# A layer's second feed-forward block: its left sums read the whole normalised activation from copies instead of rejoining its two parts

## The chip, the cores and the metric

The kernel runs on one core of a Trainium2 chip. Its time is the device time of one execution in microseconds (us). The core has a matrix engine (TensorE, PE in the profile), a vector engine (VectorE, DVE), a scalar engine (ScalarE, ACT), a general engine (GpSimd, POOL), and SyncE (SP), which here only issues DMAs, one after the other. Each engine works through its own instructions in a fixed order; an instruction that must wait for another engine or for a DMA holds up all that stand behind it on its engine.

## The reference

One decoder layer for 1024 tokens of width 1024 in float32. The second feed-forward block, cut out of the whole, is

```
h = modulate(rms_norm(x, ffn2_norm[l]), sh3, sc3)
x = x + 0.5 * g3[:, None, :] * swiglu(h, ffn2_w_gate[l], ffn2_w_up[l], ffn2_w_down[l])
return rms_norm(x, final_norm)
```

with `modulate(h, shift, scale) = h * (1 + scale) + shift` and `swiglu(h, wg, wu, wd) = (silu(h @ wg) * (h @ wu)) @ wd`, and 2816 hidden channels. Ahead of it stand a first block of the same form and a mixer (a gated convolution and a state-space model) whose output projection ends in the kernel's w_out.

## The kernel before

The tokens are worked on in two halves of 512 (h = 0 and 1), the width in 8 k-tiles of 128. A tile of 128x512 float32 is 256 KB. Every factor of a matrix product is split into a high part hi (rounded to the matrix engine's short float32 form, fp32r) and a low part lo = value − hi, and one product of two tiles is three matmuls, hi·hi, hi·lo and lo·hi (`mm3`). ScalarE makes the hi parts (a cast), VectorE the lo parts (a subtraction).

The hidden channels are 11 groups of 256. Group 0 of the second block (`group0`, names fb0g for gate products, fb0u for up products) uses plain products, because it can start on half 0 while half 1 is still being normalised. Groups 1 to 10 (`seven`, names fb1g, fb1u and so on) multiply a 2x2 block matrix by seven products in place of eight. The left blocks are A11 and A12 (half 0, k-tiles 0 to 3 and 4 to 7), A21 and A22 (half 1, likewise), and four sums: S1 = A21 + A22, S2 = S1 − A11, S3 = A11 − A21, S4 = A12 − S2. The sums are made once and then serve ten groups.

The sums are made by `combos` and `combos_last`, on VectorE, from the parts of h: each block's tile is first made whole again by adding hi and lo (`whole`, names f, and s for S2), then added or subtracted, then split into hi (ScalarE, names h3S) and lo (VectorE). That is 9 VectorE instructions for each of four k, and 4 more for S4, 52 in all, with 16 casts on ScalarE. Before that `modulated` makes h for each k-tile and half: VectorE computes t = x · scale · 1/rms, ScalarE writes hi = t + shift, and VectorE writes lo = (t + shift) − hi in one three-operand instruction (SCALAR_TENSOR_TENSOR).

`seven("fb1", ...)` calls, after its first product (fb1gA, with A11), the down projection of group 0: `down2`, names fb0d. It has 16 outputs of 128x512, each of two `mm3`, 96 matmuls together. Each output stands in one of a few PSUM banks until VectorE has added it to the residual stream (`x <- fb0d, gate, x`); only then is the bank free for a later output. After fb0d come fb1gC (with S1), fb1gB (S2), fb1gD (S3), fb1gA (A12), fb1gE (A22) and fb1gC again (S4).

What sets the order: `Clock` counts the `mm3` issued and lets side work, the generators `combos` among it, advance by a step every few of them; an instruction scheduler then puts each engine's instructions in a final order. `Weights` loads weights in pieces of 1 MB (names raw), in order, as buffers come free; ScalarE casts a piece and VectorE makes its low part (names w). The temporaries of 128x512 (t, f, s and others) come from one pool (`t2k`) of six buffers used in turn. DMAs are all issued by SP in program order.

Of the kernel before, what the change touches and what calls it, by code (L numbers as in the profile page):

```python
# [13 lines left out]
F32 = mybir.dt.float32  # L14
F32R = mybir.dt.float32r
I32 = mybir.dt.int32
AF = mybir.ActivationFunctionType
ALU = mybir.AluOpType
# [3 lines left out]
P = 128  # L22
D = 1024
S = 1024
HALF = 512
# [207 lines left out]
def hymba_layer(ctx: ExitStack, tc, x_d, wm1_d, wmod_d, gu1_d, gs1_d, ds1_d, wl1_d, win_d, wout_d, glu_d, gu2_d, gs2_d, wd2_d, ds2_d, wl2_d, cols_d, cond_d, lam_d, bc_d, out_d):  # L233
    nc = tc.nc
    V, A, T, SP = (InOrder(tc, e) for e in (nc.vector, nc.scalar, nc.tensor, nc.sync))

    def pool(name, bufs=1, **kw):
        return ctx.enter_context(tc.tile_pool(name=name, bufs=bufs, **kw))
# [5 lines left out]
    scratch = pool("scratch", space=DRAM)  # L244
# [8 lines left out]
    def mov(name, where="A", shape=(P, 2, HALF), dtype=F32R):  # L253

        return movs[where].tile(list(shape), dtype, tag="m", name=name)
# [13 lines left out]
    def t2k(name):  # L269
        return tmp.tile([P, HALF], F32, tag="t", name=name)  # L270
# [47 lines left out]
    clock = Clock(4)  # L318
# [24 lines left out]
    def parts(name, where="A"):  # L343
        t = mov(name, where)
        return t[:, 0, :], t[:, 1, :]

    def split_act(src, name, where="A"):
        hi, lo = parts(name, where)
        A.copy(hi, src)
        V.tensor_tensor(out=lo, in0=src, in1=hi.bitcast(F32), op=ALU.subtract)  # L350
        return hi, lo
# [65 lines left out]
    def spread(rb, nm):  # L417
        bc = ps(nm + "bc")
        for i in range(rb.shape[1]):
            T.matmul(bc[:, i * P : (i + 1) * P], lhsT=rb[:, i, :], rhs=ident[:], start=True, stop=True)  # L420
        return bc

    def modulated(k, h, bc, n, name, where="A"):

        t = t2k(f"{name}t{k}_{h}")
        hi, lo = parts(f"{name}{k}_{h}", where)
        sh = mods[:, n, k : k + 1]
        V.scalar_tensor_tensor(out=t[:], in0=x[k][h], scalar=scl[:, n, k : k + 1], in1=bc[:], op0=ALU.mult, op1=ALU.mult)
        A.activation(hi, t[:], AF.Identity, bias=sh)
        V.scalar_tensor_tensor(out=lo, in0=t[:], scalar=sh, in1=hi.bitcast(F32), op0=ALU.add, op1=ALU.subtract)  # L430
        return hi, lo

    def norm_into(act, h, ss, n, name, where="A"):


        def use(bc):
            got = []
            for k in range(KT):
                clock.after(k, lambda k=k: got.append(modulated(k, h, bc, n, name, where)))
            act[h] = got  # L440

        ss.rstd(D, use, 8)
# [131 lines left out]
    blocks = {}  # L574


    def whole(pair, name, engine=nc.gpsimd):
        t = t2k(name)
        engine.tensor_tensor(out=t[:], in0=pair[0].bitcast(F32), in1=pair[1].bitcast(F32), op=ALU.add)
        return t  # L580

    def combos(act, name, homes):

        blocks.clear()
        while act[1] is None or len(act[1]) < KT:
            yield
        (a11, a12), (a21, a22) = [(act[h][:4], act[h][4:]) for h in range(2)]
        blocks.update(A11=a11, A12=a12, A22=a22, S1=[], S2=[], S3=[], S4=[])
        for k in range(4):
            f22, f21, f11 = whole(a22[k], f"f22_{k}", V), whole(a21[k], f"f21_{k}", V), whole(a11[k], f"f11_{k}", V)  # L590
            V.tensor_tensor(out=f22[:], in0=f21[:], in1=f22[:], op=ALU.add)
            blocks["S1"].append(split_act(f22[:], f"{name}S1_{k}", homes[0]))
            yield
            V.tensor_tensor(out=f21[:], in0=f11[:], in1=f21[:], op=ALU.subtract)
            V.tensor_tensor(out=f11[:], in0=f22[:], in1=f11[:], op=ALU.subtract)
            blocks["S2"].append(split_act(f11[:], f"{name}S2_{k}", homes[1]))
            yield
            blocks["S3"].append(split_act(f21[:], f"{name}S3_{k}", homes[2]))
            yield

    def combos_last(act, name, home):

        while "S3" not in blocks or len(blocks["S3"]) < 4:
            yield
        for k in range(4):
            f12, s2 = whole(act[0][4 + k], f"f12_{k}", V), whole(blocks["S2"][k], f"s2_{k}", V)
            V.tensor_tensor(out=f12[:], in0=f12[:], in1=s2[:], op=ALU.subtract)
            blocks["S4"].append(split_act(f12[:], f"{name}S4_{k}", home))
            yield

    SEVEN = (("A11", "A"), ("S1", "C"), ("S2", "B"), ("S3", "D"), ("A12", "A"), ("A22", "E"), ("S4", "C"))
# [224 lines left out]
    for h in range(2):  # L836
        bc = spread(rbs[h], f"p{h}")
# [10 lines left out]
    for k in range(KT):  # L848
# [4 lines left out]
        sh = mods[:, 0, k : k + 1]  # L853
        for h in range(2):
            hi, lo = parts(f"h1{k}_{h}")
# [353 lines left out]
    def after1(d, h):  # L1209
        n2[h].add(x[d][h], beside=d < 6)  # L1210
        if d == KT - 1:
            norm_into(act2, h, n2[h], 1, "h2")
# [298 lines left out]
    n3 = [Sumsq(f"n3{c}", home=acc_in_mov) for c in "ab"]  # L1511
    act3 = [None, None]
# [43 lines left out]
    mods_open.close()  # L1556
    es2.close()
    movs["B"] = ctx.enter_context(tc.tile_pool(name="movB", bufs=12))
    norm_into(act3, 0, n3[0], 2, "h3", "B")
    ws.retire(ring1)  # L1560
    for ds in ((4, 5), (6, 7)):
        w_out(ds, 1, 0)
        w_out(ds, 1, 1)
        ws.free(2)
    norm_into(act3, 1, n3[1], 2, "h3", "A")
    ring1_open.close()


# [4 lines left out]
    def group0():  # L1573

        a_tiles, pg, pu = {}, {}, {}
        g0, u0, g1 = ws.take(3)
        ready(act3, 0, KT)
        pg[0, 0], pu[0, 0] = proj(g0, act3[0], "fb0g0_0"), proj(u0, act3[0], "fb0u0_0")
        gu_evac(0, 0, pg[0, 0], pu[0, 0], a_tiles, "fb0_0_0")
        pg[1, 0] = proj(g1, act3[0], "fb0g1_0")  # L1580
        ready(act3, 1, KT)
        pg[0, 1] = proj(g0, act3[1], "fb0g0_1")
        ws.free()
        pu[0, 1] = proj(u0, act3[1], "fb0u0_1")
        gu_evac(0, 1, pg[0, 1], pu[0, 1], a_tiles, "fb0_0_1")
        ws.free()
        pg[1, 1] = proj(g1, act3[1], "fb0g1_1")
        ws.free()
        (u1,) = ws.take()
        for h in range(2):  # L1590
            gu_evac(1, h, pg[1, h], proj(u1, act3[h], f"fb0u1_{h}"), a_tiles, f"fb0_1_{h}")
        ws.free()
        return a_tiles

    clock.side.extend([combos(act3, "h3", "BAA"), combos_last(act3, "h3", "A")])
    a_prev = group0()
    kept = {g: kept_for(g, g not in LAST[1], True) for g in range(1, NGRP - 1)}
    HOMES = dict(A11="B", S2="A", A12="B", S3="A", S1="B", A22="A", S4="A")
# [132 lines left out]
```

## Time and profile before

| | us |
|---|---|
| median of 3 timed runs (lowest, highest) | 1735.42 (1735.38, 1735.46) |
| the profiled execution | 1740.78 |
| its span, from the first to the last instruction | 1739.0 |
| TensorE busy | 1665.4 (96%) |
| VectorE busy | 1273.6 (73%) |
| ScalarE busy | 596.7 (34%) |
| GpSimd busy | 375.9 (22%) |
| granted TensorE clock, mean over the span | 0.987 |

Line numbers say little here: nearly all instructions are recorded by a helper at L108, so groups are told apart by the names of their tiles, written out<-in with buffer numbers left out. The second feed-forward block starts at about 1066 us (fb0g, half 0); its half 1 starts at 1079 (fb0g), group 0's down projection fb0d at 1114.37, and fb1gC at 1145.84. In a timeline row the first number is the start and the second the length; in brackets stands how long the engine had been idle and who released it. A row of windows gives, for a stretch of time, the busy time and the instructions of TensorE's matmuls, its weight loads, VectorE, ScalarE and GpSimd, then the granted clock, the share of the DMA engines in use, and GB/s.

### The profile page before, as it was taken

How to read it: one execution, taken by the hardware profiler on the slowest of the kernel's cores; microseconds unless marked ns; L12 is line 12 of the kernel's file. 1: busy time of each engine (PE TensorE's matmuls, PEld its weight loads, DVE VectorE, ACT ScalarE, POOL GpSimd, SP SyncE). 2: the span in 40 equal slices, each digit the busy share in tenths (PEclk: the TensorE clock that was granted, in tenths of full speed). 3: DMA queues.
4: the chain of work that ended last, by engine and by line, in shares of the span. 5: the costliest groups of instructions: out<-in, count | busy, mean ns of one | idle time of the engine just before them, and what ended most of it. 6: DMA issues, size and time to landing. Idle time of an engine off the chain costs nothing.

```text
span 1739.0 us, 20621 instructions
## 1 busy us (share of the span) xinstructions
PE 1665.4 (96%) x7484; PEld 1368.4 (79%) x7484; DVE 1273.6 (73%) x2014; ACT 596.7 (34%) x1016; POOL 375.9 (22%) x290
## 2 busy tenths in 40 slices
PE   4999999999999999999999999999999999999997
PEld 3787788878878878787777778778888888888886
DVE  7939699997589997634556977967777766676656
ACT  4225433333364332331113414424444443322221
POOL 0012233322322222100000022123223322333211
PEclk9999999999999999999999999999999999999998
DMA  8222464554464656134655450114445334659312
GB/s 326 78 99 91 146 217 150 158 183 150 182 224 147 230 198 238 53 98 142 198 152 155 134 182 25 49 49 157 167 187 186 152 145 170 248 236 365 119 49 97
DMA packets 98167, 275.17 MB, mean 158 GB/s; under 512 B 18961, under 2 KB 34577, under 8 KB 86930
## 3 DMA queue, kind: packets, MB, share of 16 engines
q1 hardware_dynamic: 98066, 273.86, 44.8%
q8 instruction: 59, 0.97, 0.2%
q14 instruction: 42, 0.34, 0.1%
HBM read 194.65 MB, written 74.97 MB: 155 GB/s over the span
## 4 chain that ended last, share of the span: by engine, by line
PE 46%; DVE 7%; DMA 3%; issue 1%; ACT 0%; SPq 0%; POOL 0%; DVEq 0%; ACTq 0%
PE wo L108 2%; PE fb10d L108 2%; PE u L108 2%; PE fbd_1B L108 2%; PE fbd_0B L108 2%; PE b L108 2%; DMA swz<-si 1%; PE v L108 1%; PE fb0g L108 1%; PE fbd_1C L108 1%; PE fbd_0C L108 1%; PE fbd_1A L108 1%; PE fbd_0A L108 1%; DVE x L108 1%; DMA wm<-in_wmod 1%; PE gl L108 1%
## 5 line engine op out<-in xcount | busy, mean ns | idle before, releaser
L108 ACT CAST w<-raw 128x512 fp32r<-128x512 f32 (+1 forms) x374 | 240.4, 677 | 475.8 <-issue 79.4
L108 DVE TENSOR_TENSOR w<-raw,w 128x512 fp32r<-128x512 f32 (+1 forms) x374 | 306.6, 839 | 122.3 <-ACT w L108 121.7
L174 POOL TENSOR_TENSOR raw<-sums,raw 128x512 f32<-128x512 f32 x54 | 80.4, 1490 | 416.4 <-DVE w L108 404.0
L165 POOL TENSOR_TENSOR sums<-raw 128x512 f32<-128x512 f32 x54 | 77.4, 1434 | 335.5 <-DMA raw<-in_gs 140.8
L176 POOL TENSOR_TENSOR raw<-raw 128x512 f32<-128x512 f32 x54 | 84.7, 1571 | 96.5 <-DVE w L108 96.5
L166 POOL TENSOR_TENSOR raw<-raw 128x512 f32<-128x512 f32 x54 | 85.3, 1579 | 4.2
L108 DVE CUSTOM_DVE_ANT_0 wm<-wm,cact 128x1024 f32<-128x1024 f32 x56 | 77.6, 1398 | 10.6 <-DMA wm<-in_wmod 10.5
L367 POOL TENSOR_TENSOR n3aq<-n3aq,n3aq 128x512 f32<-128x512 f32 x5 | 7.7, 1530 | 281.3 <-ACT n3aq L108 281.1
L108 PE MATMUL p<-h,w 128*128 128x512 f32 x192 | 48.5, 415 | 8.2 <-DVE h L108 5.4
L108 DVE TENSOR_TENSOR w<-sums,w 128x512 fp32r<-128x512 f32 x54 | 52.7, 988 | 3.0 <-ACT w L108 2.4
L108 PEld LDWEIGHTS p<-h,w 128*128 128x128 f32 x192 | 38.4, 202 | 18.0 <-DVE h L108 6.4
L108 PE MATMUL wo<-oa,w 128*128 128x512 f32 x192 | 46.0, 392 | 1.2 <-DVE w L108 0.7
L108 PE MATMUL v<-h,w 128*128 128x512 f32 x192 | 46.8, 395 | 0.0
L108 PE MATMUL c<-h,w 128*128 128x512 f32 x192 | 46.6, 394 | 0.0
L108 PE MATMUL u<-h,w 128*128 128x512 f32 x192 | 46.3, 401 | 0.2 <-DVE h L108 0.2
L108 PE MATMUL b<-h,w 128*128 128x512 f32 x192 | 45.6, 393 | 0.0
L108 PE MATMUL wo<-ob,w 128*128 128x512 f32 x192 | 45.3, 391 | 0.0
L108 ACT CAST w<-sums 128x512 fp32r<-128x512 f32 x54 | 32.8, 620 | 35.2 <-PE fa9gE L108 2.2
L108 PEld LDWEIGHTS u<-h,w 128*128 128x128 f32 x192 | 36.7, 193 | 8.6 <-DVE h L108 0.6
L108 PEld LDWEIGHTS wo<-oa,w 128*128 128x128 f32 x192 | 35.7, 188 | 9.6 <-DVE w L108 1.1
L108 PEld LDWEIGHTS wo<-ob,w 128*128 128x128 f32 x192 | 35.8, 188 | 7.3
L108 PEld LDWEIGHTS b<-h,w 128*128 128x128 f32 x192 | 35.5, 188 | 7.2
(1576 smaller groups left out, 4013.1 us busy)
## 6 DMA issues: line engine op xcount, KB each, us to landing
raw<-in_gs SPq DMA_DIRECT2D x38, 1024.0 KB, 5.2
wm<-in_wmod SPq DMA_DIRECT2D x56, 512.0 KB, 4.8
raw<-in_ds SPq DMA_DIRECT2D x16, 1024.0 KB, 6.0
mw<-in_wm SPq DMA_DIRECT2D x8, 1024.0 KB, 12.8
x<-in_x SPq DMA_DIRECT2D x16, 512.0 KB, 8.5
raw<-in_win SPq DMA_DIRECT2D x8, 1024.0 KB, 5.1
raw<-in_gu SPq DMA_DIRECT2D x6, 1024.0 KB, 10.0
raw<-in_wl SPq DMA_DIRECT2D x5, 1024.0 KB, 6.5
```

The costliest lines, as they stand in the source:

```text
L108: r = getattr(self.engine, name)(*args, **kw)
L165: self.G.tensor_tensor(out=f, in0=r[2], in1=r[1], op=ALU.subtract)
L166: self.G.tensor_tensor(out=r[1], in0=r[1], in1=r[0], op=ALU.subtract)
L174: self.G.tensor_tensor(out=r, in0=s["t3"], in1=r, op=ALU.add)
L176: self.G.tensor_tensor(out=r, in0=self.chunk(j, 3), in1=r, op=ALU.subtract)
L367: nc.gpsimd.tensor_tensor(out=a, in0=a, in1=sq[:, :n], op=ALU.add)
```

## The change

`modulated` gets a destination `copied`. With it, ScalarE adds the shift in place (t becomes whole h), a DMA issued by SP copies t into a tile in which a sum's parts will stand later (half 1 into the tiles of S1, half 0 into those of S2; k-tiles 0 to 3 into a tile's first half, 4 to 7 into its second), ScalarE casts t into hi, and VectorE makes lo = t − hi as a plain subtraction. `combos3` takes the place of `combos` and `combos_last`. For each k it makes S1, S3, S2 and S4 by four VectorE instructions straight from the copies, splits S1 and S2 over the copies they were read from, and S3 into a tile of its own. S4 has no tile yet: it is sent to DRAM (s4_d), and when S1 to S3 are done it is loaded into the low half of its own tile, and split there. Each k has 8 VectorE instructions, 32 in all. New DMAs: 16 copies, 4 saves and 4 loads of 256 KB; new on ScalarE: 16 casts.

```diff
-    def modulated(k, h, bc, n, name, where="A"):
+    def modulated(k, h, bc, n, name, where="A", copied=None):
         t = t2k(f"{name}t{k}_{h}")
         hi, lo = parts(f"{name}{k}_{h}", where)
         sh = mods[:, n, k : k + 1]
         V.scalar_tensor_tensor(out=t[:], in0=x[k][h], scalar=scl[:, n, k : k + 1], in1=bc[:], op0=ALU.mult, op1=ALU.mult)
+        if copied:
+            A.activation(t[:], t[:], AF.Identity, bias=sh)
+            SP.dma_start(copied(k, h), t[:])
+            A.copy(hi, t[:])
+            V.tensor_tensor(out=lo, in0=t[:], in1=hi.bitcast(F32), op=ALU.subtract)
+            return hi, lo
         A.activation(hi, t[:], AF.Identity, bias=sh)
         V.scalar_tensor_tensor(out=lo, in0=t[:], scalar=sh, in1=hi.bitcast(F32), op0=ALU.add, op1=ALU.subtract)
         return hi, lo
...
-    def combos(act, name, homes):
+    lefts3 = {"S1": [], "S2": []}
+    def copied3(k, h):
+        left, i = {(1, 0): ("S1", 0), (1, 1): ("S1", 1), (0, 0): ("S2", 0), (0, 1): ("S2", 1)}[h, k // 4]
+        if i == 0:
+            lefts3[left].append(mov(f"h3{left}_{k}", dict(S1="B", S2="A")[left]))
+        return lefts3[left][k % 4][:, i, :].bitcast(F32)
+
+    def combos3(act):
...
+        saved = scratch.tile([4, P, HALF], F32, name="s4_d")
+        def split_into(left, tile, src):
+            hi, lo = tile[:, 0, :], tile[:, 1, :]
+            A.copy(hi, src)
+            V.tensor_tensor(out=lo, in0=src, in1=hi.bitcast(F32), op=ALU.subtract)
+            blocks[left].append((hi, lo))
         for k in range(4):
-            f22, f21, f11 = whole(a22[k], f"f22_{k}", V), whole(a21[k], f"f21_{k}", V), whole(a11[k], f"f11_{k}", V)
-            V.tensor_tensor(out=f22[:], in0=f21[:], in1=f22[:], op=ALU.add)
-            blocks["S1"].append(split_act(f22[:], f"{name}S1_{k}", homes[0]))
+            s1, s3, s2, s4 = (t2k(f"h3w{i}_{k}")[:] for i in (1, 3, 2, 4))
+            t1, t2 = (lefts3[left][k] for left in ("S1", "S2"))
+            f21, f22, f11, f12 = (t[:, i, :].bitcast(F32) for t in (t1, t2) for i in range(2))
+            V.tensor_tensor(out=s1, in0=f21, in1=f22, op=ALU.add)
+            V.tensor_tensor(out=s3, in0=f11, in1=f21, op=ALU.subtract)
+            split_into("S1", t1, s1)
             yield
-            V.tensor_tensor(out=f21[:], in0=f11[:], in1=f21[:], op=ALU.subtract)
-            V.tensor_tensor(out=f11[:], in0=f22[:], in1=f11[:], op=ALU.subtract)
-            blocks["S2"].append(split_act(f11[:], f"{name}S2_{k}", homes[1]))
+            V.tensor_tensor(out=s2, in0=s1, in1=f11, op=ALU.subtract)
+            V.tensor_tensor(out=s4, in0=f12, in1=s2, op=ALU.subtract)
+            SP.dma_start(saved[k], s4)
+            split_into("S2", t2, s2)
             yield
-            blocks["S3"].append(split_act(f21[:], f"{name}S3_{k}", homes[2]))
+            split_into("S3", mov(f"h3S3_{k}"), s3)
             yield
-    def combos_last(act, name, home):
...
         for k in range(4):
-            f12, s2 = whole(act[0][4 + k], f"f12_{k}", V), whole(blocks["S2"][k], f"s2_{k}", V)
-            V.tensor_tensor(out=f12[:], in0=f12[:], in1=s2[:], op=ALU.subtract)
-            blocks["S4"].append(split_act(f12[:], f"{name}S4_{k}", home))
+            t = mov(f"h3S4_{k}")
+            hi, lo = t[:, 0, :], t[:, 1, :]
+            SP.dma_start(lo.bitcast(F32), saved[k])
+            split_into("S4", t, lo.bitcast(F32))
             yield
...
-    norm_into(act3, 0, n3[0], 2, "h3", "B")
+    norm_into(act3, 0, n3[0], 2, "h3", "B", copied3)
...
-    norm_into(act3, 1, n3[1], 2, "h3", "A")
+    norm_into(act3, 1, n3[1], 2, "h3", "A", copied3)
...
-    clock.side.extend([combos(act3, "h3", "BAA"), combos_last(act3, "h3", "A")])
+    clock.side.append(combos3(act3))
```

VectorE's order around the first updates of the down projection, before the change. A row is an operation with out<-in and the shape; x_0_3793 is the residual tile of half 0 that the first two outputs of fb0d go to, fb_1_1a is the low part of group 0's activation for half 1, f and s are tiles made whole, h3S a sum's parts, w and raw weights:

```order
L108 TENSOR_TENSOR w_8743<-raw_8557,w_8743 128x1024
L108 TENSOR_TENSOR h3S_3_8727<-f_3_8707,h3S_3_8727 128x512
L108 TENSOR_TENSOR fb_1_1a<-fb_1_1af,fb_1_1a 128x512
L108 TENSOR_TENSOR h3S_3_8823<-f_3_8705,h3S_3_8823 128x512
L108 SCALAR_TENSOR_TENSOR x_0_3793<-fb0d_0_8834,gate,x_0_3793 128x512
L108 SCALAR_TENSOR_TENSOR x_0_3793<-fb0d_0_8842,gate,x_0_3793 128x512
L108 TENSOR_TENSOR f_0_8857<-h_0_8283 128x512
L108 TENSOR_TENSOR s_0_8859<-h3S_0_8530 128x512
L108 SCALAR_TENSOR_TENSOR x_0_3794<-fb0d_0_8850,gate,x_0_3794 128x512
L108 TENSOR_TENSOR f_0_8857<-f_0_8857,s_0_8859 128x512
L108 SCALAR_TENSOR_TENSOR x_0_3794<-fb0d_0_8866,gate,x_0_3794 128x512
L108 TENSOR_TENSOR f_1_8881<-h_0_8291 128x512
```

The same place after the change (h3w are the whole sums):

```order
L108 SCALAR_TENSOR_TENSOR x_0_3793<-fb0d_0_8867,gate,x_0_3793 128x512
L108 TENSOR_TENSOR fb_1_1a<-fb_1_1af,fb_1_1a 128x512
L108 TENSOR_TENSOR h3S_3_8856<-h3w_3_8739,h3S_3_8856 128x512
L108 SCALAR_TENSOR_TENSOR x_0_3793<-fb0d_0_8879,gate,x_0_3793 128x512
L108 SCALAR_TENSOR_TENSOR x_0_3794<-fb0d_0_8887,gate,x_0_3794 128x512
L108 SCALAR_TENSOR_TENSOR x_0_3794<-fb0d_0_8899,gate,x_0_3794 128x512
L108 TENSOR_TENSOR h3S_0_8874<-h3S_0_8874 128x512
L108 SCALAR_TENSOR_TENSOR x_1_3797<-fb0d_1_8907,gate,x_1_3797 128x512
L108 TENSOR_TENSOR h3S_1_8894<-h3S_1_8894 128x512
L108 TENSOR_TENSOR h3S_2_8914<-h3S_2_8914 128x512
L108 SCALAR_TENSOR_TENSOR x_1_3797<-fb0d_1_8919,gate,x_1_3797 128x512
L108 TENSOR_TENSOR h3S_3_8934<-h3S_3_8934 128x512
```

Between the updates stood three instructions for each k of S4 (f, s and their difference) and its lo; now only the lo stands there, and the first update has moved ahead of the last low part of the activation.

ScalarE's order where half 1 is normalised, after the change; before it, each k-tile had the one instruction `ACTIVATE h<-h3t,mods`:

```order
L108 ACTIVATE h3t_1_8456<-h3t_1_8456,mods 128x512
L108 ACTIVATE h3t_1_8467<-h3t_1_8467,mods 128x512
L108 CAST h_1_8457<-h3t_1_8456 128x512
L108 CAST h_1_8468<-h3t_1_8467 128x512
L108 CAST fb_0_0a<-fb_0_0af 128x512
L108 ACTIVATE h3t_1_8486<-h3t_1_8486,mods 128x512
L108 ACTIVATE h3t_1_8497<-h3t_1_8497,mods 128x512
```

Each tile's activation is followed by a cast, in pairs at first and one by one from the fifth k-tile on.

SP's order after the change, from the last copy of half 1 to the weight load behind S4's loads. Before it, only the weight loads in_wd and in_gs stood here:

```order
L108 DMA h3S_3_8501<-h3t_1_8538 128x512
L108 DMA s_d<-h3w_0_8549 128x512
L108 DMA raw_8596<-in_wd 128x2048
L108 DMA s_d<-h3w_1_8608 128x512
L108 DMA s_d<-h3w_2_8677 128x512
L108 DMA s_d<-h3w_3_8741 128x512
L108 DMA raw_8779<-in_gs 128x2048
L108 DMA h3S_0_8874<-s_d 128x512
L108 DMA h3S_1_8894<-s_d 128x512
L108 DMA h3S_2_8914<-s_d 128x512
L108 DMA h3S_3_8934<-s_d 128x512
L108 DMA raw_9044<-in_gs 128x2048
```

The eight copies of each half, the first save and the other three stand in one queue with the loads of weights, each ahead of the load that follows it.

More of the change, by code (lines that the diff above doesn't have):

```diff
@@ L431, in modulated, with norm_into @@
         return hi, lo
-    def norm_into(act, h, ss, n, name, where="A"):
+    def norm_into(act, h, ss, n, name, where="A", copied=None):
         def use(bc):
@@ L438, in use @@
             for k in range(KT):
-                clock.after(k, lambda k=k: got.append(modulated(k, h, bc, n, name, where)))
+                clock.after(k, lambda k=k: got.append(modulated(k, h, bc, n, name, where, copied)))
             act[h] = got
@@ L588, in combos @@
         blocks.update(A11=a11, A12=a12, A22=a22, S1=[], S2=[], S3=[], S4=[])
-        for k in range(4):
-            f22, f21, f11 = whole(a22[k], f"f22_{k}", V), whole(a21[k], f"f21_{k}", V), whole(a11[k], f"f11_{k}", V)
-            V.tensor_tensor(out=f22[:], in0=f21[:], in1=f22[:], op=ALU.add)
-            blocks["S1"].append(split_act(f22[:], f"{name}S1_{k}", homes[0]))
+        saved = scratch.tile([4, P, HALF], F32, name="s4_d")
[4 more added lines that the diff above has]
+            blocks[left].append((hi, lo))
+        for k in range(4):
+            s1, s3, s2, s4 = (t2k(f"h3w{i}_{k}")[:] for i in (1, 3, 2, 4))
[4 more added lines that the diff above has]
+            split_into("S1", t1, s1)
             yield
-            V.tensor_tensor(out=f21[:], in0=f11[:], in1=f21[:], op=ALU.subtract)
-            V.tensor_tensor(out=f11[:], in0=f22[:], in1=f11[:], op=ALU.subtract)
-            blocks["S2"].append(split_act(f11[:], f"{name}S2_{k}", homes[1]))
+            V.tensor_tensor(out=s2, in0=s1, in1=f11, op=ALU.subtract)
+            V.tensor_tensor(out=s4, in0=f12, in1=s2, op=ALU.subtract)
+            SP.dma_start(saved[k], s4)
+            split_into("S2", t2, s2)
             yield
-            blocks["S3"].append(split_act(f21[:], f"{name}S3_{k}", homes[2]))
-            yield
-    def combos_last(act, name, home):
-        while "S3" not in blocks or len(blocks["S3"]) < 4:
+            split_into("S3", mov(f"h3S3_{k}"), s3)
             yield
         for k in range(4):
-            f12, s2 = whole(act[0][4 + k], f"f12_{k}", V), whole(blocks["S2"][k], f"s2_{k}", V)
-            V.tensor_tensor(out=f12[:], in0=f12[:], in1=s2[:], op=ALU.subtract)
-            blocks["S4"].append(split_act(f12[:], f"{name}S4_{k}", home))
+            t = mov(f"h3S4_{k}")
+            hi, lo = t[:, 0, :], t[:, 1, :]
+            SP.dma_start(lo.bitcast(F32), saved[k])
+            split_into("S4", t, lo.bitcast(F32))
             yield
```

## The prediction, made before the changed kernel was run

> **What bounds the kernel now.** I read the waits of TensorE first, from the start of FFN2 to the end of the span, because TensorE is busy 96% of the span and only its gaps can be won. Each row is total us, count, longest:
>
> ```profile
> PE fb0d L108 <- DVE x L108: 5.2, 4, 2.1
> PE n_256bc L108 <- DVE n_256rb L108: 3.9, 1, 3.9
> PE n_0bc L108 <- DVE n_0rb L108: 1.9, 1, 1.9
> PE fb0d L108 <- DVE fb_0a L108: 0.6, 1, 0.6
> PE fb0d L108 <- DVE fb_1a L108: 0.4, 1, 0.4
> ```
>
> The two n_ rows belong to the final norm, which the change leaves alone. The rest, 6.2 us in six waits, is one place: the down projection of group 0 (fb0d), which runs between the first and second products of group 1. Its timeline (start, length, instructions):
>
> ```profile
> 1111.65 2.88 PE L108 MATMUL fb1gA<-h,w 128*128 128x512 f32 x12
> 1114.37 1.43 PE L108 MATMUL fb0d<-fb_0a,w 128*128 128x512 f32 x5
> ...
> 1140.03 5.97 PE L108 MATMUL fb0d<-fb_1a,w 128*128 128x512 f32 x18 [1.87 <-DVE x L108]
> 1145.84 2.88 PE L108 MATMUL fb1gC<-h3S,w 128*128 128x512 f32 x12
> 1148.56 2.88 PE L108 MATMUL fb1gB<-h3S,w 128*128 128x512 f32 x12
> ```
>
> Twelve matmuls take 2.72 us when nothing is in the way (1148.56 − 1145.84). The 96 of fb0d should take 8 × 2.72 = 21.76 us; they take 1145.84 − 1114.37 = 31.47. So **9.71 us** are lost here: the 6.2 us of waits, the refill after each, and a clock that fell at the end. The last column but two of the windows is the granted clock:
>
> ```profile
> 1096.00:1114.40 18.40, 18.40 (x83) 15.23 (x82) 18.17 (x28) 8.88 (x16) 1.29 (x1) 1.00 0.16 57
> 1128.00:1137.00 9.00, 6.24 (x26) 4.51 (x25) 9.00 (x14) 2.38 (x4) 1.51 (x1) 1.00 0.00 0
> 1140.00:1146.00 6.00, 5.97 (x19) 4.77 (x20) 5.54 (x8) 0.62 (x1) 0.44 (x1) 0.72 0.00 0
> 1160.00:1500.00 340.00, 340.00 (x1502) 281.62 (x1501) 242.09 (x352) 139.19 (x248) 101.24 (x70) 1.00 0.44 167
> ```
>
> Over those 6 us 0.72 of the clock was granted, about 6 × 0.28 = 1.7 us of the 9.71. The same rows give the culprit: VectorE (third figure) is busy 18.17 of 18.40 us before fb0d and 9.00 of 9.00 inside it. From 1160 on TensorE has no gap and VectorE is at 71%. The chain of waits says what VectorE was doing:
>
> ```profile
> 1102.02 0.53 ACT h3S L108
> ...
> 1105.55 0.60 DVE f L108
> ...
> 1130.06 0.60 DVE s L108
> 1130.66 0.66 DVE x L108
> ```
>
> From 1102.57 to the end of fb0d this chain is VectorE alone: the residual update x, which empties a PSUM bank for TensorE, stands in VectorE's queue behind the making of the left sums (f, s, h3S). These pieces also give the step from one instruction to the next: 0.60 us for a 128x512 add, 0.66 for the three-operand form.
>
> **What the change removes.** VectorE's groups between 1078 and 1146 (busy, mean ns):
>
> ```profile
> L108 DVE TENSOR_TENSOR h3S<-f,h3S 128x512 fp32r<-128x512 f32 x16 | 12.9, 817 | 0.2 <-ACT h3S L108 0.2
> L108 DVE TENSOR_TENSOR f<-h 128x512 f32<-128x512 f32 x16 | 10.9, 709 | 0.0
> L108 DVE SCALAR_TENSOR_TENSOR x<-fb0d,gate,x 128x512 f32<-128x512 f32 x15 | 10.7, 737 | 0.0
> L108 DVE TENSOR_TENSOR f<-f,f 128x512 f32<-128x512 f32 x12 | 8.2, 682 | 0.0
> ...
> L108 DVE SCALAR_TENSOR_TENSOR h<-h3t,mods,h 128x512 fp32r<-128x512 f32 x8 | 5.6, 746 | 0.0
> ...
> L108 DVE TENSOR_TENSOR f<-f,s 128x512 f32<-128x512 f32 x4 | 3.1, 779 | 0.0
> L108 DVE TENSOR_TENSOR s<-h3S 128x512 f32<-128x512 f32 x4 | 2.7, 679 | 0.0
> ```
>
> The sums cost 16 + 16 + 12 + 4 + 4 = 52 instructions now. The change needs 8 for each of four k: 32. The 20 that only rejoined hi and lo are gone: 20 × 0.60 = 12.0 us. The low parts of h change from the three-operand form to a subtraction, 8 × 0.06 = 0.5 us more in this half. Order matters as much: up to fb0d's first update VectorE has 27 sum instructions instead of 35, and among the updates only 5 instead of 17 (three S4 subtractions per k become one, and only one S3 remains).
>
> **Does 12 us suffice?** I replayed VectorE's new order with these steps, each instruction at the later of its turn and its input. VectorE's row for the last low part of group 0's activation is now
>
> ```profile
> 1121.58 0.68 DVE L108 TENSOR_TENSOR fb_1a<-fb_1af,fb_1a 128x512 fp32r<-128x512 f32 x1
> ```
>
> so it is ready at 1122.2; in the new order it comes near 1117.3, and TensorE, undelayed, asks for it at 1120.5. In fb0d TensorE then hands over a bank each 1.36 us, 21.8 us for 16; VectorE has 16 × 0.66 + 9 × 0.60 = 16 us of work there (5 sums, about 4 weight parts). Each bank is free at least 2.8 us before it is asked for. All six waits go, with refill and clock: **−9.7 us**. VectorE keeps some 5 us in hand, so it need not gain the full 12.
>
> **What it adds: ScalarE and the copies.** Whole h is written in place, then cast: 8 casts more per half. ScalarE's groups from 1054 to 1146, and the rows of the second half, where TensorE follows closely:
>
> ```profile
> L108 ACT ACTIVATE h<-h3t,mods 128x512 fp32r<-128x512 f32 x16 | 11.0, 724 | 13.7 <-DVE h3t L108 13.6
> L108 ACT CAST h3S<-f 128x512 fp32r<-128x512 f32 x16 | 9.7, 620 | 24.2 <-DVE f L108 24.2
> ```
> ```profile
> 1079.29 1.38 ACT L108 ACTIVATE h<-h3t,mods 128x512 fp32r<-128x512 f32 x2 [5.43 <-DVE h3t L108]
> ...
> 1088.30 2.07 DVE L108 SCALAR_TENSOR_TENSOR h<-h3t,mods,h 128x512 fp32r<-128x512 f32 x3
> ...
> 1090.79 1.98 PE L108 MATMUL fb0g<-h,w 128*128 128x512 f32 x8
> ```
>
> A pair of activations takes 1.38, so 0.69 each; a cast 0.53 (the chain's row). Eight tiles cost ScalarE 8 × 1.22 = 9.8 us from 1079.29, plus one activation's cast: done about 1090.4, the last low part about 1091.1 instead of 1090.3. TensorE uses it at the end of the row of eight, near 1092.5. Tile by tile the slack stays about 1.5 us: nothing lost, at most 0.5 if each cast has to wait for the write before it. In the first half (1054 to 1071) the last part is ready about 2 us early; over both halves ScalarE idles for 13.6 us behind VectorE's h3t (its row), which takes the 8 × 0.53 more.
>
> The copies are the unknown. Six temporaries rotate; a tile is free again only when its copy has landed. No 256 KB copy within the chip's memory is in the trace. The nearest rows (KB, median us to landing), and the longest of the kind in the chain:
>
> ```profile
> mi_d<-mi SPq DMA_DIRECT2D x8, 256.0 KB, 2.3
> mi<-mi_d SPq DMA_DIRECT2D x8, 256.0 KB, 3.6
> swz<-si SPq DMA_DIRECT2D x16, 128.0 KB, 2.9
> ...
> raw<-in_wd SPq DMA_DIRECT2D x1, 1024.0 KB, 4.8
> ```
> ```profile
> 888.79 7.14 DMA swz<-si
> ```
>
> Bounds 2.3 and 7.1; I take 3, since the queue is almost empty here (the windows show 1 to 57 GB/s against the 167 carried later). The first copy of the second half leaves near 1080.1, and VectorE wants that tile again for the sixth k near 1085: up to 5 us nothing waits. At 7.1 TensorE loses 7.1 − 5.0 = 2.1 us, up to 3 with the first half's 1 us: 1728.7.
>
> SP issues in order; the copies stand ahead of weight loads:
>
> ```profile
> 1095.15 0.33 SPq L108 DMA_DIRECT2D raw<-in_wd  x1
> 1121.12 0.33 SPq L108 DMA_DIRECT2D raw<-in_gs  x1
> ```
>
> The load of in_wd (used by fb0d) waits for a VectorE weight part that I place 1.6 us later, so about 1096.7; landing 4.8 us on, 1101.5, is ahead of its use at 1114. The next load gets earlier, about 1114.5. Four S4 loads follow it, land by 1122 and are used at 1159.44 + 9.7 less; their four casts stand in ScalarE's queue ahead of weight parts needed after 1136. Landing as late as 10 us would cost under 1 us, by holding the S4 subtractions in front of x.
>
> **Sum.** The profiled execution took 1740.78 us (span 1739.0 and 1.8 around it): 1740.78 − 9.7 = 1731.1. The three timed runs stand 5.36 lower, at 1735.42, and which part of the span is shorter there is not shown; I take the same difference: 1735.42 − 9.7 = **1725.7 us**.
>
> A page speaks against the last 1.7 us of this. The Trainium skill ("TensorE: Matmul & The Clock Gate", Part 1: The HAM clock gate) says that the clock halves after an idle window of about 3.4 us. No wait here is longer than 2.1 us, and yet the clock fell where the waits are, so the rows differ from a strict reading of the page. By the page the fall has another cause and stays, and the sum is 1727.4; by the rows it goes with the waits, 1725.7.
>
> **The rivals.**
> *Part stays* (0.10). Copies land near 7 us, or the sixth temporary and S4 hold VectorE in turn: the 2 to 3 us above, plus the clock's 1.7, 1728 to 1731. For it: the 7.14 row; against it: the median 2.9 and the idle queue.
> *Nothing* (0.05). VectorE still ends last because what it saves it waits for elsewhere, on ScalarE's casts: 13.6 us of idling moved into its queue. Then fb0d keeps its 31 us, about 1735. Against it: ScalarE is busy 8.88 of 18.40 us before fb0d, so it can take eight casts.
> *Slower* (0.05). The six temporaries, held by slow copies: from a landing of 5 us on, each us delays TensorE by one in the second half, and from about 7 on by another in the first. At 9 us this costs 4 + 2 = 6; break-even with 9.7 is near 11; at 12 us it is 7 + 5 = 12, and the time 1737.7. The landings of 256 KB between 2.3 and 3.6 speak against it.
> *Forecast* (0.80): all of fb0d's loss goes, 1723.5 to 1728.
>
> **How the numbers follow.** Likeliest 1725.7. The range, 1723 to 1731, holds the forecast and the first rival, and leaves out "nothing" and "slower" with 0.10; its low end allows 2.7 us for a loss that is larger in the timed runs than in the profiled one. A measurement of this kernel tells about 0.2% (3.5 us) from no change, so faster means below 1731.9: forecast and first rival, 0.90; same 0.05, slower 0.05.
>
> **What would show it.** In the changed profile: no fb0d wait on x, fb_0a or fb_1a; fb0d about 21.8 us from its first matmul to fb1gC; the clock 1.00 there; VectorE's sums 32 instructions after h and idle time inside fb0d; the copies at 2.3 to 3.6 us; no wait of fb0g or fb0u on h. Wrong would be: fb0g waiting on h, VectorE's h3t waiting for a copy, or fb0d still waiting on x behind h3S.

## The result

The changed kernel took a median of 1729.35 us (1725.27 to 1734.43, 10 runs). The kernel before, run beside it on the same chips, took 1740.01 (1735.38 to 1743.89, 10 runs), 4.6 us more than the three runs the prediction started from. The ratio is 0.9941, with a 95% interval of 0.9928 to 0.9954: 10.2 us faster, 8.0 to 12.5. The forecast was 9.7 us, a ratio of 0.9944, and 1725.7 us, with a range of 1723 to 1731.

### The profile page after: what moved, and what is told of

It is laid out like the page before. It is cut to its first block, busy times and chain, and to the rows that moved or that the text cites. A ratio compares the mean times of both kernels' runs of the same rounds, so it can differ in the third digit from the quotient of the medians.

```text
span 1727.0 us, 20694 instructions
## 1 busy us (share of the span) xinstructions
PE 1661.6 (96%) x7484; PEld 1368.2 (79%) x7484; DVE 1263.0 (73%) x1994; ACT 604.6 (35%) x1032; POOL 373.8 (22%) x290
## 4 chain that ended last, share of the span: by engine, by line
PE 48%; DVE 5%; DMA 3%; issue 1%; ACT 0%; SPq 0%; POOL 0%; DVEq 0%; ACTq 0%
PE wo L108 2%; PE fb10d L108 2%; PE u L108 2%; PE fbd_1B L108 2%; PE fbd_0B L108 2%; PE b L108 2%; PE v L108 1%; DMA swz<-si 1%; PE fb0u L108 1%; PE fbd_0A L108 1%; PE fb0g L108 1%; PE fbd_1C L108 1%; PE fbd_0C L108 1%; PE fbd_1A L108 1%; PE fb0d L108 1%; DMA wm<-in_wmod 1%
## 5 line engine op out<-in xcount | busy, mean ns | idle before, releaser
L108 DVE CUSTOM_DVE_ANT_0 wm<-wm,cact 128x1024 f32<-128x1024 f32 x56 | 78.1, 1408 | 10.3 <-DMA wm<-in_wmod 10.2
## 6 DMA issues: line engine op xcount, KB each, us to landing
raw<-in_gu SPq DMA_DIRECT2D x6, 1024.0 KB, 10.2
```

Of the source, the lines that this page charges most:

```text
L108: r = getattr(self.engine, name)(*args, **kw)
```

## The profile after

The waits of TensorE from 1050 us to the end of the changed kernel's span, the whole answer (total us, count, longest):

```profile
PE n_256bc L108 <- DVE n_256rb L108: 3.5, 1, 3.5
PE n_0bc L108 <- DVE n_0rb L108: 1.9, 1, 1.9
```

The six waits of fb0d are gone, and none has taken their place. The timeline of TensorE in the changed kernel:

```profile
1063.90 5.60 PE L108 MATMUL fb0g<-h,w 128*128 128x512 f32 x24
...
1112.00 5.60 PE L108 MATMUL fb0d<-fb_0a,w 128*128 128x512 f32 x24
1117.44 5.60 PE L108 MATMUL fb0d<-fb_1a,w 128*128 128x512 f32 x24
1122.88 5.60 PE L108 MATMUL fb0d<-fb_0a,w 128*128 128x512 f32 x24
1128.32 5.60 PE L108 MATMUL fb0d<-fb_1a,w 128*128 128x512 f32 x24
1133.76 2.88 PE L108 MATMUL fb1gC<-h3S,w 128*128 128x512 f32 x12
```

fb0d takes 1133.76 − 1112.00 = 21.76 us in place of 31.47, which is 96 matmuls at the undisturbed pace. The spans differ by more, 1739.0 − 1727.0 = 12.0 us. The other 2.37 are there before the change begins: the statistics of half 0's norm (n3ast) start on TensorE at 1045.65 in place of 1048.02, ahead of the first copy at 1054.06, and fb0g at 1063.90 in place of 1066.27. From fb0g to fb0d both kernels take 48.10 us, and from fb1gC to the end 593.16 before and 593.24 now. Two further profiles of the kernel before (below) start fb0g at 1063.31 and 1060.52, so that this part of the span varies by 6 us between executions of one kernel, and a comparison of two spans alone could be wrong by as much.

The windows of the changed kernel (busy time of TensorE, weight loads, VectorE, ScalarE, GpSimd; granted clock; DMA share; GB/s), before and inside fb0d, answer to those of the prediction:

```profile
1094.00:1112.00 18.00, 18.00 (x81) 14.88 (x80) 17.97 (x28) 9.48 (x16) 2.21 (x1) 1.00 0.25 94
1112.00:1134.00 22.00, 22.00 (x99) 18.21 (x98) 17.50 (x27) 5.44 (x10) 4.68 (x3) 1.00 0.29 102
```

VectorE is as full as before ahead of fb0d, but inside it 4.5 us are idle, and the clock is 1.00. VectorE's own timeline shows who waits for whom now:

```profile
1120.25 0.69 DVE L108 TENSOR_TENSOR h3S<-h3S 128x512 fp32r<-128x512 f32 x1 [1.86 <-ACT h3S L108]
...
1131.24 0.75 DVE L108 SCALAR_TENSOR_TENSOR x<-fb0d,gate,x 128x512 f32<-128x512 f32 x1 [0.61 <-PE fb0d L108]
1132.60 0.75 DVE L108 SCALAR_TENSOR_TENSOR x<-fb0d,gate,x 128x512 f32<-128x512 f32 x1 [0.61 <-PE fb0d L108]
1133.96 0.75 DVE L108 SCALAR_TENSOR_TENSOR x<-fb0d,gate,x 128x512 f32<-128x512 f32 x1 [0.61 <-PE fb0d L108]
```

The last updates come every 1.36 us, each behind TensorE: the roles are exchanged. The first of the rows is the price of the trip by DRAM, a wait of VectorE for S4's cast, which ScalarE could not make before the load had landed:

```profile
1119.60 2.46 ACT L108 CAST h3S<-h3S 128x512 fp32r<-128x512 f32 x4 [4.66 <-DMA h3S<-s_d]
```

The new transfers, in the DMA issues of the changed kernel (KB, median us to landing):

```profile
h3S<-h3t SPq DMA_DIRECT2D x16, 256.0 KB, 2.3
...
s_d<-h3w SPq DMA_DIRECT2D x4, 256.0 KB, 2.0
...
h3S<-s_d SPq DMA_DIRECT2D x4, 256.0 KB, 6.5
```

## The experiments

Two questions were open. Is the gain the number of VectorE's instructions, or the place from which S4's were taken? And do the copies, the casts and the trip by DRAM cost anything that the gain hides? Those that were timed repeatedly have a ratio to the kernel before on the same chip; the others were run once. Where a few us matter, the length of fb0d in the profile (its first matmul to fb1gC) is sharper: in three profiles of the kernel before it was 31.47, 31.47 and 31.61 us.

**The 20 instructions put back into the changed kernel.** Their results are not used.

```diff
+            V.tensor_tensor(out=s1, in0=f21, in1=f22, op=ALU.add)
+            V.tensor_tensor(out=s1, in0=f21, in1=f22, op=ALU.add)
             V.tensor_tensor(out=s1, in0=f21, in1=f22, op=ALU.add)
+            V.tensor_tensor(out=s3, in0=f11, in1=f21, op=ALU.subtract)
             V.tensor_tensor(out=s3, in0=f11, in1=f21, op=ALU.subtract)
...
         for k in range(4):
+            whole(act[0][4 + k], f"f12_{k}", V), whole(blocks["S2"][k], f"s2_{k}", V)
             t = mov(f"h3S4_{k}")
```

> The changed kernel with 20 VectorE additions put back whose results are not used: for each k, S1's sum is made twice more and S3's once more, and at S4 a tile of A12 and one of S2 are made whole. Theory 'load and place' (VectorE is late in fb0d, partly by its count of instructions, partly because S4's work stood between the updates of x): about half of the loss comes back, fb0d 26 to 28 us in place of 21.8, waits on fb_0a, fb_1a and x reappear, time 0.9965 to 0.998 of the kernel before. Theory 'count alone': all of it comes back, fb0d near 31.5 us, ratio 0.999 to 1.001. Theory 'place alone': nothing comes back, 0.994.

Measured: ratio 0.9997 (0.9983 to 1.0011), 1737.69 us. TensorE's waits near fb0d in this kernel:

```profile
PE fb0d L108 <- DVE x L108: 3.5, 5, 0.8
PE fb0d L108 <- ACT fb_1sg L108: 0.8, 1, 0.8
PE fb0d L108 <- DVE fb_1af L108: 0.2, 1, 0.2
PE fb0d L108 <- DVE fb_1a L108: 0.2, 1, 0.2
```

Its timeline, the first row of fb0d and the row behind it, and its window over fb0d:

```profile
1111.43 4.58 PE L108 MATMUL fb0d<-fb_0a,w 128*128 128x512 f32 x18
...
1140.97 2.88 PE L108 MATMUL fb1gC<-h3S,w 128*128 128x512 f32 x12
```
```profile
1110.00:1142.00 32.00, 27.16 (x109) 19.24 (x108) 31.36 (x48) 9.57 (x18) 4.56 (x3) 1.00 0.24 82
```

fb0d takes 29.54 us: 7.78 of the 9.71 come back. "Place alone" falls. "About half" was too low; the time is what "count alone" expected, and fb0d stays 1.9 us under the 31.5 of the kernel before, about the 1.7 us of clock: here the granted clock is 1.00 throughout.

**Only S4's place changed, in the kernel before.** Still 52 instructions, no copy, no DRAM.

```diff
-    clock.side.extend([combos(act3, "h3", "BAA"), combos_last(act3, "h3", "A")])
+    clock.side.append(combos(act3, "h3", "BAA"))
...
-    seven("fb1", lambda: down2(a_prev, 2, "fb0", (0, 1)), 0, kept[1])
+    def between():
+        down2(a_prev, 2, "fb0", (0, 1))
+        clock.side.append(combos_last(act3, "h3", "A"))
+
+    seven("fb1", between, 0, kept[1])
```

> The kernel before with one thing changed: the side work that makes S4 is entered only after fb0d has been issued, so its 16 VectorE instructions no longer stand between the first updates of x; no copy, no DRAM, still 52 instructions. Theory 'load and place': the waits on x mostly go, those on fb_0a and fb_1a (1.0 us) and the first x (0.5) stay: fb0d about 23.5 us in place of 31.5, ratio 0.995 to 0.996. Theory 'count alone' (the 20 instructions must go): the delay only moves to the end of fb0d or to fb1gC's S4, ratio 0.998 to 1.001.

Measured: ratio 0.9984 (0.9965 to 1.0002), 1734.41 us. Timeline of TensorE, its first and last rows of fb0d and the product with S4:

```profile
1116.47 1.42 PE L108 MATMUL fb0d<-fb_0a,w 128*128 128x512 f32 x5
1118.46 4.59 PE L108 MATMUL fb0d<-fb_0a,w 128*128 128x512 f32 x19 [0.58 <-DVE fb_0a L108]
...
1140.75 2.88 PE L108 MATMUL fb1gC<-h3S,w 128*128 128x512 f32 x12
...
1154.35 2.20 PE L108 MATMUL fb1gC<-h3S,w 128*128 128x512 f32 x9
1157.54 0.50 PE L108 MATMUL fb1gC<-h3S,w 128*128 128x512 f32 x1 [0.98 <-ACT h3S L108]
...
1158.83 2.89 PE L108 MATMUL fb1uA<-h,w 128*128 128x512 f32 x12
```

fb0d is 24.28 us, so 7.2 of the 9.7 us go without a single instruction less, 1.7 of them clock (it is 1.00 here): "count alone" is wrong about fb0d. About what comes behind it, that theory was right. It expected the delay to move to fb1gC's S4, and the product with S4 takes 4.48 us in place of 2.72, because the last S4 tile is now late there: 1.76 us come back. By the profile 5.4 us remain (0.9969). By the times 2.8 us remain, with an interval from 6.1 us to none, so the times alone do not tell this kernel from the one before. Their ratio lies in the range of "count alone" (0.998 to 1.001), and the 0.995 to 0.996 of "load and place" was too good; what speaks for "load and place" is the length of fb0d.

**S4 the old way in the changed kernel.** Copies as in the change; S4 from A12 and S2 made whole, no trip by DRAM. The subtraction that made S4 for that trip and its save are left out too.

```diff
...
-            t = mov(f"h3S4_{k}")
-            hi, lo = t[:, 0, :], t[:, 1, :]
-            SP.dma_start(lo.bitcast(F32), saved[k])
-            split_into("S4", t, lo.bitcast(F32))
+            f12, s2 = whole(act[0][4 + k], f"f12_{k}", V), whole(blocks["S2"][k], f"s2_{k}", V)
+            V.tensor_tensor(out=f12[:], in0=f12[:], in1=s2[:], op=ALU.subtract)
+            blocks["S4"].append(split_act(f12[:], f"h3S4_{k}", "A"))
```

> The changed kernel with S4 made the old way, after S1 to S3: A12 and S2 made whole by VectorE, subtracted, split; no trip by DRAM. 40 VectorE instructions in place of 32, 16 of them after the start of fb0d in place of 4. Theory 'load and place': VectorE enters fb0d in time (no wait on fb_0a or fb_1a), and its 16 S4 instructions take 9.6 us beside 10.6 of updates and 2 to 4 of other work in 21.8 us: waits on x of 0 to 1.5 us, fb0d 21.8 to 23.5. Theory 'S4's place is what counts': fb0d 27 us or more.

Measured, one run: 1729.83 us. TensorE waits once:

```profile
1111.60 5.60 PE L108 MATMUL fb0d<-fb_0a,w 128*128 128x512 f32 x24
...
1130.30 4.38 PE L108 MATMUL fb0d<-fb_1a,w 128*128 128x512 f32 x18 [0.67 <-DVE x L108]
1134.52 2.88 PE L108 MATMUL fb1gC<-h3S,w 128*128 128x512 f32 x12
```

22.92 us: the whole detour by DRAM is worth 1.2 of the 9.7 us, since VectorE enters fb0d in time.

**How much VectorE has in hand.** Eight unused additions (4.8 us), once ahead of fb0d (S1's and S3's sums made twice) and once inside it (the `whole` line of the first experiment). The first of the two:

```diff
+            V.tensor_tensor(out=s1, in0=f21, in1=f22, op=ALU.add)
             V.tensor_tensor(out=s1, in0=f21, in1=f22, op=ALU.add)
+            V.tensor_tensor(out=s3, in0=f11, in1=f21, op=ALU.subtract)
             V.tensor_tensor(out=s3, in0=f11, in1=f21, op=ALU.subtract)
```

> The changed kernel with 8 unused additions on VectorE ahead of fb0d (S1's and S3's sums made twice), 4.8 us. The prediction said that VectorE keeps some 5 us in hand. If so fb0d takes 21.8 to 22.5 us (at most a wait of 0.6 on fb_1a). If VectorE has nothing in hand: 26 us.

> The changed kernel with 8 unused additions on VectorE at S4 (A12 and S2 made whole), 4.8 us inside fb0d. With some 4 us of idle time inside fb0d by the changed kernel's trace: fb0d 21.8 to 22.5 us, no wait on fb_0a or fb_1a. If place alone decides: several waits on x, fb0d 25 us or more.

Measured, one run each, 1730.72 and 1732.03 us: fb0d takes 22.95 and 23.35 us, with one wait each, on x, of 0.9 and 0.8 us. TensorE's first row of fb0d and the row behind it, first with the additions ahead of fb0d, then inside it:

```profile
1112.84 5.60 PE L108 MATMUL fb0d<-fb_0a,w 128*128 128x512 f32 x24
...
1135.79 2.88 PE L108 MATMUL fb1gC<-h3S,w 128*128 128x512 f32 x12
```
```profile
1113.65 5.60 PE L108 MATMUL fb0d<-fb_0a,w 128*128 128x512 f32 x24
...
1137.00 2.88 PE L108 MATMUL fb1gC<-h3S,w 128*128 128x512 f32 x12
```

Both lie a little above the 22.5 that was expected of a reserve of 5 us, and far under a reserve of none. Taken together, with the work put back over the changed kernel and the loss of fb0d over 21.76:

| kernel | VectorE work more than the change (us) | fb0d (us) | lost (us) | in hand: work − loss |
|---|---|---|---|---|
| 8 ahead of fb0d | 8 × 0.60 = 4.8 | 22.95 | 1.19 | 3.6 |
| 8 inside | 4.8 | 23.35 | 1.59 | 3.2 |
| S4 the old way | 4.8 | 22.92 | 1.16 | 3.6 |
| 20 put back | 12.0 | 29.54 | 7.78 | 4.2 |
| copies only (next) | 12.0 | 29.50 | 7.74 | 4.3 |
| kernel before, without its 1.7 us of clock | 12.5 | 29.8 | 8.0 | 4.5 |

One rule fits all six: TensorE loses what VectorE is given beyond some 3 to 4.5 us. The place matters in the same way: S4's work behind the updates (the second experiment) is work taken out of VectorE's queue ahead of them.

**The copies and casts alone.** The changed kernel with the sums made the old way; nothing reads the copies.

```diff
...
-            V.tensor_tensor(out=s1, in0=f21, in1=f22, op=ALU.add)
-            V.tensor_tensor(out=s3, in0=f11, in1=f21, op=ALU.subtract)
-            split_into("S1", t1, s1)
+            f22, f21, f11 = whole(a22[k], f"f22_{k}", V), whole(a21[k], f"f21_{k}", V), whole(a11[k], f"f11_{k}", V)
+            V.tensor_tensor(out=f22[:], in0=f21[:], in1=f22[:], op=ALU.add)
+            split_into("S1", lefts3["S1"][k], f22[:])
...
```

> The changed kernel with the sums made the old way: whole h by ScalarE, the 16 copies and the extra casts stay, but nothing reads the copies; the tiles are made whole by VectorE's additions again (52 instructions) and S4 does not go by DRAM. It prices the copies and the casts alone. Theory of the prediction (they cost nothing, the gain is VectorE's alone): ratio 0.998 to 1.000, fb0d 29 to 32 us, no wait of fb0g or fb0u on h. Rival (copies or casts cost something that the gain hides): above 1.001, with waits on h. Second rival (the copies' kernel gains by its h path): below 0.997.

Measured: ratio 0.9996 (0.9978 to 1.0014), 1737.56 us; the only waits are on x (the timeline rows below give fb0d 29.50 us):

```profile
PE fb0d L108 <- DVE x L108: 5.9, 5, 2.5
```
```profile
1111.20 5.60 PE L108 MATMUL fb0d<-fb_0a,w 128*128 128x512 f32 x24
...
1140.70 2.88 PE L108 MATMUL fb1gC<-h3S,w 128*128 128x512 f32 x12
```

No wait of fb0g or fb0u on h, and from fb0g to fb0d 48.10 us as in the kernel before (1063.10 to 1111.20): 16 copies of 256 KB and 16 casts cost nothing here, and gain nothing either. Without the 1.7 us of clock the kernel before takes 29.8 us for fb0d; this one takes 29.50, at a clock of 1.00.

**Each copy three times,** meant to price slow copies.

```diff
-            SP.dma_start(copied(k, h), t[:])
+            to = copied(k, h)
+            for _ in range(3):
+                SP.dma_start(to, t[:])
```

> The changed kernel with each of the 16 copies issued three times to the same place, so that a temporary is free only when the third has landed: the price of slow copies. By the prediction's rule (no wait up to a landing of 5 us, then one us of TensorE for each us more in the second half, and from 7 on in the first half too): if the third copy lands 4 to 5 us after its issue turn, no wait and ratio 0.994; at 8 us a loss of 3 + 1, ratio 0.9963. Rival 'copies never matter': ratio 0.994 and no wait of fb0g on h even if the third lands after 7 us. Rival 'copies are dear': waits on h of more than 8 us, ratio over 0.999.

Measured: ratio 0.9971 (0.9960 to 0.9982), 1735.33 us, so about 5 us of the gain are lost. A window of it, the copies among the DMA issues (KB, median us to landing), then rows of the timelines of SP, ScalarE, VectorE and TensorE:

```profile
1060.00:1075.00 15.00, 14.91 (x71) 12.19 (x70) 12.49 (x25) 10.55 (x16) 0.00 (x0) 1.00 0.98 364
```
```profile
h3S<-h3t SPq DMA_DIRECT2D x48, 256.0 KB, 2.5
```
```profile
1072.54 22.93 SPq L108 DMA_DIRECT2D h3S<-h3t  x25
```
```profile
1095.09 2.09 ACT L108 CAST w<-raw 128x1024 fp32r<-128x1024 f32 x3 [3.22 <-PE fb0g L108]
```
```profile
1096.17 2.43 DVE L108 TENSOR_TENSOR w<-raw,w 128x1024 fp32r<-128x1024 f32 x3 [3.58 <-ACT w L108]
1098.52 1.78 DVE L108 TENSOR_TENSOR h3w<-h3S 128x512 f32<-128x512 f32 x1
```
```profile
1113.02 0.84 PE L108 MATMUL fb0d<-fb_0a,w 128*128 128x512 f32 x3
...
1138.65 2.88 PE L108 MATMUL fb1gC<-h3S,w 128*128 128x512 f32 x12
```

The DMA engines are full in the first half (98%, 364 GB/s), and the second half's copies leave SP one each 0.92 us (22.93 / 25) until 1095. But they land hardly later than single ones: 2.5 us in the median, 6.4 at most. The third copy of a tile thus lands some 4.3 us after the first one's turn (2 × 0.92 + 2.5, an estimate), for which the expectation was no wait and 0.994. It missed: fb0g and fb0u do not wait for h, and VectorE waits only once, 0.29 us, for a copy to free a temporary, yet fb0d takes 25.63 us, 3.87 too many. VectorE's first sum comes at 1098.5 in place of 1086.2 (in the changed kernel). It idles 3.58 us just before, for ScalarE's cast of a weight, which itself waited 3.22 us for TensorE; neither wait is ended by a copy. The order on VectorE is another in this kernel: the weight part now stands ahead of the first sum. So landings beyond 5 us were not tested here, and how much of the loss is the copies' and how much the order's was not measured.

**The additions on GpSimd instead,** in the kernel before; no copies.

```diff
-            f22, f21, f11 = whole(a22[k], f"f22_{k}", V), whole(a21[k], f"f21_{k}", V), whole(a11[k], f"f11_{k}", V)
+            f22, f21, f11 = whole(a22[k], f"f22_{k}"), whole(a21[k], f"f21_{k}"), whole(a11[k], f"f11_{k}")
...
-            f12, s2 = whole(act[0][4 + k], f"f12_{k}", V), whole(blocks["S2"][k], f"s2_{k}", V)
+            f12, s2 = whole(act[0][4 + k], f"f12_{k}"), whole(blocks["S2"][k], f"s2_{k}")
```

> The kernel before with the 20 additions that make tiles whole moved from VectorE to GpSimd; no copies. Theory 'VectorE's instructions are all that counts': the same gain as the change, ratio 0.994 to 0.996. Theory 'contention': in the trace of before a VectorE sum that runs beside a GpSimd addition takes 1.77 us in place of 0.68 (start 1102.57 beside GpSimd's 1102.51), so each moved addition takes from VectorE about 1.1 us to spare it 0.6: 20 x 0.5 = 10 us more of delay in the same stretch, ratio 1.002 to 1.008, with VectorE's means for sums above 0.9 us.

Measured: ratio 1.0020 (1.0004 to 1.0037), 1741.78 us, slower. A group of VectorE and one of GpSimd from 1076 to 1146 (busy us, mean ns), a timeline row of each that lie beside each other in time, TensorE's first row of fb0d and the row behind it, and a window over fb0d:

```profile
L108 DVE TENSOR_TENSOR h3S<-f,h3S 128x512 fp32r<-128x512 f32 x16 | 15.3, 972 | 0.2
```
```profile
L579 POOL TENSOR_TENSOR f<-h 128x512 f32<-128x512 f32 x16 | 26.7, 1685 | 21.8 <-DVE h L108 8.1 <-DVE f L108 7.1 <-DVE h3S L108 6.6
```
```profile
1098.15 5.69 POOL L579 TENSOR_TENSOR f<-h 128x512 f32<-128x512 f32 x3 [4.78 <-DVE h3S L108]
```
```profile
1100.91 3.48 DVE L108 TENSOR_TENSOR w<-raw,w 128x512 fp32r<-128x512 f32 x2
```
```profile
1112.95 1.37 PE L108 MATMUL fb0d<-fb_0a,w 128*128 128x512 f32 x4
...
1145.37 2.88 PE L108 MATMUL fb1gC<-h3S,w 128*128 128x512 f32 x12
```
```profile
1110.00:1142.00 32.00, 26.40 (x96) 19.37 (x95) 31.68 (x38) 9.49 (x16) 21.59 (x13) 0.89 0.10 33
```

Two subtractions of weights (0.68 each alone) take 3.48 us beside GpSimd's additions. The Trainium skill ("SBUF — State Buffer", Who interferes with whom) says that a VectorE instruction with two inputs in SBUF contends with a GpSimd instruction that reads SBUF, and that the one that comes second waits for the whole of the other. The rows here agree: three additions take GpSimd 5.69 us, 1.90 each, which is about one by itself (1.28 at the shortest) and one step of VectorE (0.60).

From fb0g to fb1gC this kernel takes 81.56 us (1063.81 to 1145.37) against 79.57 before. That is 2.0 us more, and not the 10 that "contention" expected; the times say 3.5 (0.7 to 6.4). fb0d takes 32.42 us, though TensorE has only three waits in it, 2.2, 2.1 and 1.1 us. The clock is the other part: 0.89 over the window's 32 us costs 3.5 us, against 1.7 in the kernel before. So VectorE lost about as much to waiting inside other instructions as the 20 additions had taken, and most of the 2.0 us is clock: without it the two kernels take 78.1 and 77.9 us. Whether the clock falls as often in other executions of this kernel was not measured. That GpSimd is idle most of the time is not room for this work.

**The kernel before, profiled twice more.**

> The kernel before, unchanged, profiled once more: is the loss in fb0d (31.47 us in place of 21.76) the same in another execution, and its clock of 0.72 after the waits? Theory 'the waits are fixed by the order and the fall of the clock goes with them': fb0d 31.0 to 31.9 us, granted clock below 0.9 in the 6 us ahead of fb1gC. Theory 'the fall is a coincidence of one execution': the same six waits, fb0d 29.5 to 30.2 us, clock 1.00 there.

> The kernel before, unchanged, a third profile: the same question. With waits of the same size but a clock that falls in some executions only, fb0d lies at 29.5 to 30.2 or at 31.0 to 31.9 us and the six waits do not change by more than 0.2 us each.

Measured: fb0d 31.47 us (1111.41 to 1142.88) and 31.61 (1108.62 to 1140.23) with the same six waits (5.2, 0.6 and 0.4 us in both), and the clock falls both times. First a window of the second profile, then one of the third:

```profile
1136.00:1142.00 6.00, 4.93 (x15) 3.93 (x16) 6.00 (x10) 0.63 (x1) 1.48 (x1) 0.72 0.00 0
```
```profile
1136.00:1142.00 6.00, 6.00 (x21) 4.86 (x21) 5.35 (x9) 1.14 (x2) 0.00 (x0) 0.75 0.00 0
```

So the fall is no coincidence of one execution. The 0.72 and 0.75 are means: in windows of 2 us the clock goes down to 0.50 (in the first profile 0.63, 0.52 and 1.00 from 1140 to 1146), and what is missing from 1.00 adds up to 1.70 us in each of the three profiles, which is half the clock for about 3.4 us. That the waits bring it about is likely but not shown: with copies only, five waits of up to 2.55 us left the clock at 1.00, while the GpSimd kernel lost the same 1.70 us twice, beside waits of 2.1 and 2.2 us.

## Why the prediction was right, point by point

- **The place and the size of the gain.** All 9.71 us of fb0d's loss went, and the timed gain is 10.2 us (8.0 to 12.5). The replay of VectorE's order held in the steps that can be read off. Adding the 2.37 us by which this execution was early, the last low part of group 0's activation was ready at 1117.5 (forecast 1117.3), the last low part of h at 1091.1 (1091.1), the load of in_wd left at 1097.0 (1096.7), the next load at 1115.0 (1114.5), and the first of S4's loads had landed at 1122.0 (forecast: all by 1122). Two readings are slightly off, and nothing hangs on them: by the order shown ahead of the prediction, 36 sum instructions stand before the first update and 16 behind it, not 35 and 17; and the chain is VectorE's up to 1139.98, where fb0d's last 18 matmuls take over, not to the end of fb0d.
- **Why it went.** That VectorE's load ahead of the updates sets fb0d, and nothing else that came with the change, is shown: with the 20 instructions put back the gain is gone, copies read or not (0.9997 and 0.9996, each to about 0.2%; fb0d 29.54 and 29.50 us), and with S4's work moved behind the updates 7.2 us of fb0d's loss go without any copy.
- **The reserve.** "Some 5 us in hand" was too much: 3.2 to 4.5 by five experiments and the kernel before.
- **The clock's 1.7 us.** The prediction took them into the sum against a strict reading of the Trainium skill ("TensorE: Matmul & The Clock Gate", Part 1: The HAM clock gate). The measurement bears it out: no wait in fb0d is longer than 2.1 us, the fall went with the waits, and it came back in each further profile of the kernel before. That the clock falls with any such waits is not so: see below.
- **The copies.** Taken at 3 us between 2.3 and 7.1; 2.3 measured, nothing waits.
- **S4 by DRAM.** The loads took 6.5 us behind a weight load of 1 MB and held VectorE for 1.86 us, which cost TensorE nothing. The detour brings 1.2 us.
- **The rival "slower"** was not tested. With each copy made three times a temporary was free again after some 4.3 us (the estimate above), within the 5 us that the rival allows, and TensorE did not wait for h. The 3.87 us lost in fb0d came with another order on VectorE. What slower landings would cost is neither shown nor excluded.
- **The absolute time** is partly luck. At 1729.35 it lay 3.6 us above the forecast, in the stretch from 1728 to 1731 that the prediction had given to its rival "part stays"; the trace shows that nothing of the loss stayed. The three runs that the forecast started from are the lowest three of the ten of the kernel before (1735.38 to 1735.46; the other seven lie from 1737.69 to 1743.89). The time fell into the range because the range had room for the rival. As a difference the forecast missed by 0.5 us.

## What to carry to other kernels

Where an engine off TensorE's path empties the banks TensorE needs, count the work that stands in that engine's queue ahead of each emptying, over the stretch and not over the span: VectorE was at 73% on average and yet cost TensorE 9.7 us in one place. Taking work away and moving it behind the emptyings are the same remedy, and moving it took a few lines and brought 5.4 of the 9.7 us by its profile (by its times, 2.8 us, it cannot be told from no change). 1.76 us were lost where the moved work came late for its own reader. Moving it to an idle engine is only a remedy if the two do not exclude each other.

## What the runs showed of the hardware

- Copies of 256 KB within the chip's memory landed in 2.3 us (median) in the changed kernel, where the DMA engines were 33% busy (1075 to 1094). With three times as many, which kept the engines full for 15 us (98%, 364 GB/s), the median was 2.5 us and the longest 6.4.
- Beside each other, VectorE's two-input instructions went from 0.68 to as much as 1.77 us, and GpSimd's additions from 1.28 to 1.69 us in the mean.
- In the kernel before the granted clock was halved for about 3.4 us (a mean of 0.72 over 6 us, 1.7 us lost) after six waits of 0.4 to 2.1 us, 6.2 in all. In the GpSimd kernel it was so twice, with three waits in fb0d of 1.1 to 2.2 us. In the kernel with copies only it stayed at 1.00, with five waits of 0.7 to 2.55 us, 5.9 in all. What of the pattern of waits decides was not settled.
- TensorE lost more than its listed waits: 7.74 us with 5.9 us of waits, in five pieces, at full clock. Part of it is how a wait is counted: from the end of the last matmul, which lasts 0.39 us, while in an unbroken row the next one starts 0.23 us (2.72 / 12) after it.
